# Seven slots of stationary weights and seven low-part slots, moved within 256 bytes of SBUF

## The chip, the cores and the metric

The kernel runs on one NeuronCore of one Trainium2 chip; the other cores are idle. The metric is the device time of one execution in microseconds, as the median of repeated runs. All inputs and outputs are float32 in device memory.

## The reference: what is computed

One hybrid decoder layer for a sequence of 1024 tokens and a model width of 1024:

```
h = x + W_out( concat[ sliding-window attention heads with sinks | forgetting-attention heads ] )
        both head groups read RMSNorm(x) through one combined input projection
y = h + W_down( relu( W_up RMSNorm(h) )^2 )        W_up: 1024 x 4096, W_down: 4096 x 1024
```

## The kernel before

**Numbers in two parts.** TensorE multiplies in a reduced form of float32 (`float32r`). To keep float32 accuracy every operand is split into a high part (a rounded copy) and a low part (the rest), by `split` (lines 75 to 80): one engine makes the copy, another one the difference. A product of two operands is then three matmuls into one PSUM bank: high x high, high x low and low x high. A matmul instruction has a *stationary* operand (128 columns, brought in by its own weight load, LDWEIGHTS) and a *moving* operand (up to 512 columns). Every matmul of the profile has its own weight load, also where two in a row use the same weights.

**The stages.** First the input projection for part of the heads (tile `qps`, moving 384 columns), then the attention with the remaining projections threaded in between (tiles `ps`, moving 384 or 392 columns), then the output projection (`po`, moving 512), then the up projection (`pu`, moving 512) and the down projection (`pd`, moving 512). Up and down are done by Strassen-Winograd's scheme: seven products of half-size blocks instead of eight.

**The up stage** (`up`, line 1060, called for j = 0 to 15 from line 1298). For each j it takes sums and differences of four blocks of raw weights (`wur`, `wus`) on VectorE, and then, for the seven products in the order `UP = (1, 2, 3, 6, 7, 5, 4)`, it splits that product's weights into a slot `wu` and multiplies:

```
w = w_slot("wu", [2, 4, P], F32R)
split(w[:, 0], w[:, 1], src[n], nc.scalar, nc.vector if n in (2, 6, 5) else nc.gpsimd)
for k in range(4):
    mm(m[n], w[:, 0, k], bh[n][:, k], k == 0, False)
    mm(m[n], w[:, 0, k], bl[n][:, k], False, False)
    mm(m[n], w[:, 1, k], bh[n][:, k], False, k == 3)
```

So a product is 12 matmuls: four triples, each of high weights x high part, high weights x low part, low weights x high part. Seven products by 16 steps by 12 make 1344 matmuls. The moving operands `bh[n]` and `bl[n]` are made once in the output stage and stay. The weights go through seven slots `w0` to `w6` in turn (`w_slot`, line 1054, with `nw` starting at 4). Because there are seven products and seven slots, each product meets the same slot in every step: product 1 uses w5, 2 uses w6, 3 uses w0, 6 uses w1, 7 uses w2, 5 uses w3 and 4 uses w4.

**The slots.** All of these buffers come from `slot` (line 146): a named place in a pool that is given out again and again. Pool `zw` (tags w0 to w6, 4096 bytes per partition each, and two buffers `wor` of 2048 bytes) lies above pool `zl` (tags m0 to m5, r0, r1, 8192 bytes each); pool `zr` (tags c0 to c13, 8192 bytes each, then `rr` and `tmp`) lies at the other end of SBUF. Inside a pool the places follow each other in the order in which the tags are first asked for; for `zw` this is w2, w4, w3, wor twice, w0, w1, w5, w6. Tags c0, c2, ... c12 hold the high parts `bh[n]`, and c1, c3, ... c13 the low parts `bl[n]`. All these sizes are whole multiples of 256 bytes, so before the change every one of these slots starts at the same place modulo 256 bytes (224), and so do the inner pieces of a slot that matmuls read, which lie multiples of 512 bytes apart.

The slots have other users too. In the output stage w0 and w1 hold the split output weights `wos` (`out_weights`, line 870), w2 and w3 the tiles `xt` and `h`, w4 the tiles `pc` and `b12`. In the down stage w0 to w6 receive the raw hidden rows `hr` by DMA (line 1200), c0 to c9 the raw weights `wda`, c10 to c13 two of the first four pairs `hx`, `wx` of split operands (`FIRST`, line 1149: `hx` in c10 and c12, `wx` in c11 and c13), and later the sums of the results.

**One stage whose low part lies elsewhere.** In `w_tiles` (line 178) the projection weights, which are the moving operand there, have their low part 384 x 4 = 1536 bytes after the high part where 384 columns are loaded, a multiple of 256; where 392 columns are loaded it lies 400 x 4 = 1600 bytes after it, 64 bytes off a multiple of 256:

```
lo = 384 if n == 384 else 400
return wr, w[:, :n], w[:, lo : lo + n]
```

The order of the instructions on each engine is chosen when the program is built, by a planner with a cost model; waits between engines follow from which tiles are read and written. Pools are opened with `reuse_waits="tile"`: a tile that takes over bytes of an earlier tile waits for that tile's last users.

Of the kernel before, what the change touches and what calls it, by code (L numbers as in the profile page):

```python
# [16 lines left out]
P = 128  # L17
# [38 lines left out]
def hybrid_layer(  # L56
# [86 lines left out]
        tc.tile_pool(name="zl", bufs=1, side="left", reuse_waits="tile")  # L143
    )}

    def slot(tag, name, shape, dt=F32, pool=None):
        pool = o[pool or ("zw" if tag[0] == "w" else "zl")]
        return pool.tile([P] + shape, dt, tag=tag, name=name, bufs=1)


    X = [
        [slot(tag, "x", [2, 2, 512], F32R) for tag in tags]
        for tags in (("m1", "m2", "m3", "m4"), ("m0", "r0", "r1", "m5"))
    ]
# [705 lines left out]
    def mix_tiles(e):  # L860
        m = mixt[e] = slot(MIX[e], f"mix{e}", [2, S], F32R)
        mh[e], ml[e] = m[:, 0, :], m[:, 1, :]
# [7 lines left out]
    def out_weights(dt, e0):  # L870
        i = nout[0] = nout[0] + 1
        wr = o["zw"].tile([P, 4, P], F32, tag="wor", name="wor", bufs=2)
        nc.sync.dma_start(wr, w_o[dt][:, e0 : e0 + 4, :])
        w = slot(f"w{i % 2}", "wos", [2, 4, P], F32R)
        split(w[:, 0], w[:, 1], wr, nc.scalar, nc.gpsimd)
        return w[:, 0], w[:, 1]
# [154 lines left out]
    for dt in (1, 5, 2, 6, 3, 7):  # L1031
        w = out_weights(dt, 4)
# [273 lines left out]
    for i in range(len(STEPS)):  # L1306
        down(i)
        if STEPS[i][0] == len(PHASES) - 1 and late:
            name, dt, cs = late.pop(0)
# [65 lines left out]
```

## Time and profile before

| what | before |
|---|---|
| median of three runs | 1091.47 us (1091.2 to 1092.87) |
| span of the profiled execution, first to last instruction | 1090.4 us |
| what lies around the span, taken as median less span | 1.1 us |
| TensorE matmul busy | 1080.1 us, 99% of the span |
| weight loads busy (beside the matmuls) | 933.8 us, 86% |
| VectorE / ScalarE / GpSimd busy | 782.7 / 571.4 / 362.4 us |
| up stage, first to last start of a matmul | 473.7 to 780.8 us |
| granted TensorE clock | 0.999 |

The profiled execution's own device time is not listed apart from its span. Matmuls are pipelined: a row's duration of one matmul (some 390 ns) is longer than the distance from its start to the next one's start, and it is this distance that adds up to the time. It is read by dividing a stretch by the number of weight loads or matmuls that start in it.

### The profile page before, as it was taken

How to read it: one execution, taken by the hardware profiler on the slowest of the kernel's cores; microseconds unless marked ns; L12 is line 12 of the kernel's file. 1: busy time of each engine (PE TensorE's matmuls, PEld its weight loads, DVE VectorE, ACT ScalarE, POOL GpSimd, SP SyncE). 2: the span in 40 equal slices, each digit the busy share in tenths (PEclk: the TensorE clock that was granted, in tenths of full speed). 3: DMA queues.
4: the chain of work that ended last, by engine and by line, in shares of the span. 5: the costliest groups of instructions: out<-in, count | busy, mean ns of one | idle time of the engine just before them, and what ended most of it. 6: DMA issues, size and time to landing. Idle time of an engine off the chain costs nothing.

```text
span 1090.4 us, 15675 instructions
## 1 busy us (share of the span) xinstructions
PE 1080.1 (99%) x5556; PEld 933.8 (86%) x5556; DVE 782.7 (72%) x1321; ACT 571.4 (52%) x1022; POOL 362.4 (33%) x352
## 2 busy tenths in 40 slices
PE   9999999999999999999999999999999999999998
PEld 8999999999898888778888888888888888888886
DVE  8377677765776786898686869867665876674395
ACT  5558588776667766554545444353633433333331
POOL 4572523434445543333222232322212222231100
PEclk9999999999999999999999999999999999999999
DMA  9401212324657564663554543443998876665523
GB/s 292 156 22 53 69 36 65 113 70 150 230 164 252 182 209 173 212 231 126 193 184 174 188 160 135 149 170 145 335 390 308 305 288 224 237 231 177 176 87 116
DMA packets 96223, 195.69 MB, mean 179 GB/s; under 512 B 7392, under 2 KB 19856, under 8 KB 96144
## 3 DMA queue, kind: packets, MB, share of 16 engines
q1 hardware_dynamic: 95856, 194.54, 51.0%
q8 instruction: 44, 0.72, 0.3%
q14 instruction: 35, 0.29, 0.1%
q10 hardware_dynamic: 288, 0.15, 0.0%
HBM read 141.61 MB, written 53.04 MB: 179 GB/s over the span
## 4 chain that ended last, share of the span: by engine, by line
PE 86%; DMA 5%; DVE 4%; ACT 1%; issue 1%; POOL 1%; SPq 0%; DVEq 0%; ACTq 0%; POOLq 0%
PE pd L73 28%; PE pu L73 27%; PE ps L73 13%; PE po L73 4%; PE spb L73 3%; PE pvb L73 3%; PE tpb L739 3%; PE sp L73 1%; PE pv L73 1%; PE tpa L568 1%; DMA h_d<-h 1%; DMA xq<-in_x_dram 1%; DMA wr<-in_w_a_dram 1%; DMA rd_d<-rd 1%; PE ptk L334 1%
## 5 line engine op out<-in xcount | busy, mean ns | idle before, releaser
L73 PE MATMUL pd<-hx,wx 128*128 128x512 f32 (+1 forms) x1350 | 304.9, 388 | 0.0
L73 PEld LDWEIGHTS pd<-hx,wx 128*128 128x128 f32 x1350 | 252.7, 188 | 52.2
L73 PE MATMUL pu<-bh,wu 128*128 128x512 f32 x896 | 276.6, 390 | 0.3 <-POOL wu L80 0.2
L73 PEld LDWEIGHTS pu<-bh,wu 128*128 128x128 f32 x896 | 168.0, 188 | 36.1 <-POOL wu L80 0.6
L73 PE MATMUL ps<-w,x 128*128 128x384 f32 (+1 forms) x960 | 198.3, 344 | 0.5 <-ACT z L463 0.3
L73 PE MATMUL pu<-bl,wu 128*128 128x512 f32 x448 | 174.0, 389 | 0.0
L73 PEld LDWEIGHTS ps<-w,x 128*128 128x128 f32 x960 | 164.8, 189 | 3.8 <-ACT z L463 0.7
L77 ACT CAST hx<-hr 128x1024 fp32r<-128x1024 f32 x56 | 59.1, 1055 | 176.1 <-PE pd L73 170.9
L80 POOL TENSOR_TENSOR wx<-wda,wx 128x1024 fp32r<-128x1024 f32 x24 | 64.3, 2678 | 196.6 <-ACT wx L77 188.6
L80 DVE TENSOR_TENSOR hx<-hr,hx 128x1024 fp32r<-128x1024 f32 x56 | 72.5, 1302 | 72.5 <-ACT hx L77 72.5
L73 PEld LDWEIGHTS pu<-bl,wu 128*128 128x128 f32 x448 | 84.1, 188 | 17.7 <-issue 0.2
L73 PE MATMUL po<-mix,wos 128*128 128x512 f32 x384 | 94.2, 395 | 0.6 <-ACT pc L914 0.3
L73 PEld LDWEIGHTS po<-mix,wos 128*128 128x128 f32 x384 | 70.6, 188 | 15.7 <-ACT wos L77 1.1
L80 POOL TENSOR_TENSOR wu<-wus,wu 128x512 fp32r<-128x512 f32 x32 | 46.6, 1459 | 111.8 <-ACT wu L77 99.5
L80 POOL TENSOR_TENSOR wu<-wur,wu 128x512 fp32r<-128x512 f32 x32 | 44.1, 1378 | 102.7 <-ACT wu L77 100.1
L1047 DVE TENSOR_TENSOR ht<-hb 128x512 f32<-128x512 f32 x32 | 22.9, 757 | 62.8 <-ACT hb L1102 62.8
L80 POOL TENSOR_TENSOR w<-wr,w 128x384 fp32r<-128x384 f32 (+1 forms) x47 | 50.1, 1074 | 40.1 <-ACT w L77 28.6
L77 ACT CAST wu<-wus 128x512 fp32r<-128x512 f32 x64 | 37.9, 618 | 46.5 <-PE pu L73 39.2
L77 ACT CAST wx<-wda 128x1024 fp32r<-128x1024 f32 x56 | 58.5, 1049 | 6.8 <-DMA wda<-in_w_d_dram 6.5
L703 ACT ACTIVATE sb<-sb,nmb 128x128 f32<-128x128 f32 (+3 forms) x64 | 49.7, 778 | 22.1 <-DVE nmb L697 21.6
L406 DVE TENSOR_TENSOR ptl<-tpb,pth 128x512 fp32r<-128x512 f32 (+1 forms) x80 | 49.6, 631 | 15.1 <-ACT pth L405 14.3
L1101 ACT ACTIVATE hb<-hb 128x2048 f32<-128x2048 f32 x16 | 30.7, 1917 | 48.5 <-DVE hb L1050 48.4
(211 smaller groups left out, 1844.5 us busy)
## 6 DMA issues: line engine op xcount, KB each, us to landing
wda<-in_w_d_dram SPq DMA_DIRECT2D x34, 1024.0 KB, 8.7
hr<-hid_d SPq DMA_DIRECT2D x56, 512.0 KB, 5.7
wur<-in_w_u_dram SPq DMA_DIRECT2D x32, 512.0 KB, 4.4
hid_d<-ht SPq DMA_DIRECT2D x16, 1024.0 KB, 4.5
hid_d<-hb SPq DMA_DIRECT2D x16, 768.0 KB, 3.6
mix<-mixs_d SPq DMA_DIRECT2D x7, 1024.0 KB, 5.4
wr<-in_w_b_dram SPq DMA_DIRECT2D x32, 192.0 KB, 2.5
xq<-in_x_dram SPq DMA_DIRECT2D x8, 512.0 KB, 5.9
```

What stands on the lines that cost most here:

```text
L73: return nc.tensor.matmul(out, lhsT, rhs, start=start, stop=stop)
L77: hi_eng.copy(hi, src)
L80: lo_eng.tensor_tensor(out=lo, in0=src, in1=hi.bitcast(F32), op=ALU.subtract)
L334: nc.tensor.transpose(pt[:w, j * P : (j + 1) * P], x[:, 4 * c + j, col : col + w], ident)
L406: nc.vector.tensor_tensor(out=lo[:, cols], in0=pt[:, cols], in1=hi[:, cols].bitcast(F32), op=ALU.subtract)
L568: nc.tensor.transpose(tp[:, hh * P : (hh + 1) * P], pts[hh // 2][:, hh % 2, c0 : c0 + P], ident)
L703: nc.scalar.activation(pr[:, :nk], pr[:, :nk], AF.Exp, scale=-1.0, bias=nm[:, c : c + 1], accum_out=dn_b[p % 2][:, h, i : i + 1] if p < 3 ...
L739: nc.tensor.transpose(tp[:, c0 : c0 + P], probs[qi][:, kb * P : (kb + 1) * P], ident)
L1047: eng.tensor_tensor(out=out, in0=a, in1=b, op=ALU.subtract)
L1101: nc.scalar.activation(b, b, AF.Relu)
```

## The change

Four of the seven weight slots and all seven low-part slots become a little larger than what is put into them, and the contents start a little behind the slot's start:

```
+    SHIFT = {
+        "w4": 2, "w3": 4, "w1": 4, "w5": 4,
+        "c1": 16, "c3": 16, "c5": 16, "c7": 16, "c9": 16, "c11": 16, "c13": 16,
+    }
+
     def slot(tag, name, shape, dt=F32, pool=None):
         pool = o[pool or ("zw" if tag[0] == "w" else "zl")]
-        return pool.tile([P] + shape, dt, tag=tag, name=name, bufs=1)
+        if tag not in SHIFT:
+            return pool.tile([P] + shape, dt, tag=tag, name=name, bufs=1)
+        n, by = math.prod(shape), SHIFT[tag]
+        full = 1024 + 8 if tag[0] == "w" else 2048 + 64
+        t = pool.tile([P, full], dt, tag=tag, name=name, bufs=1)[:, by : by + n]
+        if len(shape) == 1:
+            return t
+        if len(shape) == 2:
+            return t.rearrange("p (a b) -> p a b", b=shape[1])
+        return t.rearrange("p (a b c) -> p a b c", b=shape[1], c=shape[2])
```

A shifted w slot is 32 bytes larger, so what follows it in the pool moves by 32 bytes. Modulo 256 bytes the slots then start, in their order in the pool, at: w2 224, w4 232 (8 bytes in), w3 16, w0 32, w1 48, w5 80, w6 96. A shifted c slot is 256 bytes larger and its contents start 64 bytes in: the low parts lie at 32 modulo 256, the high parts stay at 224. No instruction is added or taken away, none changes its shape, and each slot keeps its name, its number of buffers and its users.

## The prediction

> **What bounds the kernel now.** I read the page's header, the granted clock and the busy shares first, then the waits of TensorE.
>
> ```profile
> span 1090.4 us, 15675 instructions
> PE 1080.1 (99%) x5556; PEld 933.8 (86%) x5556; DVE 782.7 (72%) x1321; ACT 571.4 (52%) x1022; POOL 362.4 (33%) x352
> ...
> core 0: 1090.4 us, clock 0.999
> ...
> engine line waited for: us in total, times, longest us
> PE qps L73 <- DVE warm L191: 1.3, 1, 1.3
> ...
> PE pu L73 <- POOL wu L80: 0.2, 1, 0.2
> ```
>
> TensorE is busy for 99% of the span at a full clock. Its longest wait for another engine is 1.3 us, and in the up stage it waits 0.2 us in all for a split weight. So the time is the number of matmuls times the distance between two starts, and a change of places counts only by what it does to that distance. The next view is the instructions that touch the tile `wu`, then the weight loads in order of time, merged, for three stretches without a break: `qps` with 384 columns, `pd` with 512, and `ps` with 392. The last row is the up stage by windows.
>
> ```profile
> engine op xcount: duration ns min/median/max, first and last start us, forms
> L73 PEld LDWEIGHTS pu<-bh,wu x896: 186/188/190, 473.5 to 780.5; 128*128 128x128 f32 x180
> L73 PE MATMUL pu<-bh,wu x896: 388/389/793, 473.7 to 780.8; 128*128 128x512 f32 x180
> ...
> L73 PE MATMUL pu<-bl,wu x448: 387/389/396, 473.9 to 780.5; 128*128 128x512 f32 x150
> ```
>
> ```profile
> 10.91 27.75 PEld L73 LDWEIGHTS qps<-w,x 128*128 128x128 f32 x160
> ...
> 800.03 135.96 PEld L73 LDWEIGHTS pd<-hx,wx 128*128 128x128 f32 x600
> ...
> 43.35 6.95 PEld L73 LDWEIGHTS ps<-w,x 128*128 128x128 f32 x39
> ...
> 490.00:626.00 136.00, 136.00 (x602) 112.65 (x600) 103.58 (x149) 63.55 (x86) 39.76 (x29) 1.00 0.46 171
> ```
>
> A row of n weight loads lasts n - 1 distances and one load of 188 ns. For 384 columns that is (27.75 - 0.19) / 159 = 173.3 ns; for 512 in the down stage (135.96 - 0.19) / 599 = 226.7 ns; in the up stage 136.00 / 600 = 226.7 ns. The two sizes give a slope of 53.3 ns / 128 = 0.417 ns per column and a fixed part of 13.3 ns per matmul. By that rule 392 columns take 163.3 + 13.3 = 176.7 ns; measured is (6.95 - 0.19) / 38 = 177.9 ns, with some 0.3 ns of uncertainty since the row gives hundredths of a microsecond. This is the one stretch in which the low part lies 64 bytes off the high part modulo 256, by `lo = 400` in line 183. In the two others stationary and moving operands all lie at one place modulo 256.
>
> The up stage is then 1344 x 226.7 = 304.6 us of the 307.3 us from the first matmul at 473.7 to the one behind the last (780.8 + 0.2); 2.7 us are breaks at its start and in its middle. After a break the distance isn't at once 226.7 ns. The matmuls behind the one in step 10, in order of time:
>
> ```profile
> 666.30 0.79 PE L73 MATMUL pu<-bh,wu 128*128 128x512 f32 x1
> 666.93 0.40 PE L73 MATMUL pu<-bl,wu 128*128 128x512 f32 x1
> 667.17 0.63 PE L73 MATMUL pu<-bh,wu 128*128 128x512 f32 x2
> 667.63 0.39 PE L73 MATMUL pu<-bl,wu 128*128 128x512 f32 x1
> ...
> 669.02 0.39 PE L73 MATMUL pu<-bl,wu 128*128 128x512 f32 x1
> ```
>
> From 666.93 to 669.02 there are nine distances, 2.09 us, so 232 ns each: 5.5 ns more than in the settled stream, 50 ns until it has settled. The same operands at the same places thus cost 5.5 ns more when the stream isn't in step. I read the fixed 13.3 ns as partly a matter of how the reads of moving and stationary operand fall against each other, and that is what the change shifts.
>
> **The change part by part.** *Instructions.* None is added, removed or moved; the pools grow by 4 x 32 and 7 x 256 bytes per partition. Cost 0 by itself.
>
> *The low parts' shift.* 448 of the 1344 matmuls stream a low part that now lies 64 bytes off, just as in the 392-column stretch, with a triple in the same order: high, low, high. That stretch pays 177.9 - 176.7 = 1.2 ns per matmul on the average of its triple. For 1344 matmuls this is 1.6 us, if the excess comes from the 64 bytes. It may also come from the 392 columns themselves, which no other stretch has; then it is 0. The trace can't tell these apart. I take the half, **0.8 us**.
>
> *The seven stationary places.* Only product 7 (slot w2, at 224) keeps its place. For the six others no row shows a stationary operand elsewhere than at 224 beside a float32 moving operand of 512. Below, the whole fixed part could go: 13.3 ns for 6/7 of 1344 = 1152 matmuls, 15.4 us less. Above, the stream could stay out of step all the time: 5.5 ns x 1152 = 6.3 us more. The nearest row is the 392-column one, where operands do lie at two places, and its distance differs by about 1 ns from the rule. So I take 0 for them beside the 0.8 us above, and keep both ends.
>
> *The switches.* Every 12 matmuls the stationary operand goes to another place, 16 x 7 = 112 times. If the stream falls out of step each time and settles in nine matmuls, this is 112 x 50 ns = 5.6 us; if it slides over, 0. In the 392-column stretch the moving place alternates two times in three matmuls for at most 3.7 ns per triple, so a switch costs some 2 ns there: 112 x 2 ns = **0.2 us**.
>
> *Output and down stage.* Their slots move too: `wos` now lies at 32 and 48, and two `wx` at 32.
>
> ```profile
> L73 PE MATMUL po<-mix,wos 128*128 128x512 f32 x384 | 94.2, 395 | 0.6 <-ACT pc L914 0.3 <-ACT wos L77 0.3
> L73 PE MATMUL pd<-hx,wx 128*128 128x512 f32 x1338 | 303.4, 389 | 0.0
> ```
>
> That is at most 384 + 48 matmuls, against 1152; they are taken at 0 like those, with ends by their share of 432 / 1152: -5.8 to +2.4 us.
>
> *VectorE, ScalarE, GpSimd, DMA.* Splits write to the moved slots, and `hr` is loaded into them by DMA.
>
> ```profile
> L77 ACT CAST wu<-wus x64: 601/620/629, 472.2 to 759.4; 128x512 fp32r<-128x512 f32 x64
> L80 POOL TENSOR_TENSOR wu<-wus,wu x32: 1291/1426/1911, 477.8 to 757.5; 128x512 fp32r<-128x512 f32 x32
> ...
>   PE pu L73: 54.2, 29
> ...
> hr<-hid_d SPq DMA_DIRECT2D x56, 512.0 KB, 5.7
> ...
>   PE pd L73: 170.9, 49
> ```
>
> Seven slots give a split a lead of several products of 12 x 226.7 = 2.7 us; ScalarE in its turn sits idle 54.2 us until TensorE frees a slot of `wu` and 170.9 us in the down stage. A split of 0.62 + 1.43 us would have to become several times longer before TensorE waited: 0. A load of 5.7 us is issued as soon as its slot is free, so a few per cent more there cost 0 as well. If this cover were gone, each microsecond of delay per product would cost 112 us, but nothing here is near that.
>
> **Sum.** 0.8 + 0.2 + 0 = 1.0 us more than the profiled span of 1090.4, so 1091.4 us; with the 1.1 us that lie between span and median the time is 1091.47 + 1.0 = **1092.4 us**.
>
> **A rule of the skill against the trace.** The Trainium skill, page "TensorE: Matmul & The Clock Gate", section "Step-by-step: what each phase is for", says that TensorE has two independent read ports, so loading the next weights takes nothing from the running matmul's reads. By it no place could matter and the sum would be 0: 1091.5 us, the first rival below. The 232 ns of the unsettled stream and the 177.9 ns of the 392 columns speak against a strict reading of it, though neither proves that it is the place.
>
> The same page, section "Wait — 56ns, not 53.3ns?", measures 215.7 ns for 512 columns back to back, with no fresh weights. By that the most that places could win in the up stage is an estimated 1344 x 11 ns = 14.8 us, 1076.7 us.
>
> **The rivals.**
>
> *R1, places do nothing.* The distance stays 226.7 ns for every product: 1091.5 us. For it: the same 226.7 ns stands in the up and the down stage though the tiles lie many kilobytes apart. Against it: the 392-column row. It is the same verdict as my forecast.
>
> *R2, the stream falls out of step (slower).* The place is TensorE's reads in the up stage; seven stationary places against two moving ones leave no common rhythm, and the distance goes from 226.7 ns towards the 232 ns that follow a break. At 2 ns per matmul and above it decides the verdict; with half of the 5.5 ns it is 1344 x 2.75 = 3.7 us, 1095.2 us, with all of it 7.4 us, 1098.9 us. For it: the settled rhythm stands only where all places are alike, and 392 columns are above the rule. Against it: 392 columns, with two places, are nearer to settled than to unsettled.
>
> *R3, unlike places collide less (faster).* If the 13.3 ns come largely from both reads starting at the same place modulo 256, moving six of seven products apart takes a part away: a quarter of it, 3.3 ns x 1344 = 4.5 us, gives 1087.0 us; half, 6.7 ns, 9.0 us, gives 1082.5 us. For it: the fixed part is there in every stretch in which all places are alike. Against it: nothing in the trace shows a distance of settled 512-column matmuls below 226.7, and the one mixed stretch lies above.
>
> *R4, the change misses its place*: the planner orders instructions otherwise, or a slot that now overlaps another old tile waits for it. 32 bytes to 1.8 KB of shift reach at most one neighbouring tile, whose users are the finished attention; a stop there costs one product of 2.7 us plus 50 ns of settling, so 1094.2 us.
>
> **How the numbers follow.** What a measurement of this kernel can tell from no change is about 0.2%, 2.2 us, or 1.6 ns for each of 1344 matmuls. My forecast and R1 together, within that: 0.43. R2: 0.25 and R4 0.04, both slower, with 0.02 for the slower edge of the forecast: 0.31. R3: 0.26. The time is that of the forecast, 1092.4 us. Its own range is 1090.0 to 1094.0. The whole range goes down to a quarter of the fixed part (1087.0) and up to half-way between R2's two prices, 1344 x 4.1 ns = 5.5 us, 1097.0; outside lie the deep end of R3 with 0.12 and the high end of R2 with 0.07.
>
> **What would show it.** In the profile after: 600 loads of the down stage should still last 136.0 us. In the up stage the distance should be read product by product, since each has its slot: product 7 (224) shows the low parts' shift alone, products 3, 1 and 2 those of 32, 80 and 96, product 6 48, product 5 16, product 4 232. Right would be 226 to 229 ns in each, low passes not all equal to high ones, and an up stage of 307 to 310 us. R2 would show 229 to 232 ns in most products; R3 223 or less in those away from 224, with product 7 unchanged. A stage of up that begins later than 473.7 us would be R4, or the output stage's moved `wos`. My reading as a whole is wrong if products differ by more than 5 ns from each other, for then it is the place itself and not the rhythm that sets the price.

## The result and the profile after

The changed kernel takes 1100.49 us in the median (1098.99 to 1100.92, 3 runs) against 1091.47 us: a ratio of 1.0079 with a 95% interval from 1.0059 to 1.0098, 9.0 us more. The span of its profiled execution is 1098.8 us against 1090.4.

Every engine runs the same instructions in the same order in both programs, so all of it is in how long they take. This is all that TensorE waits for in the changed kernel's up stage:

```profile
PE pu L73 <- ACT bh L990: 0.3, 1, 0.3
```

The changed kernel's rows of the tiles `po`, `pu` and `pd` (shortest, median and longest duration in ns, then first and last start in us):

```profile
L73 PE MATMUL po<-mix,wos x384: 387/394/507, 332.0 to 474.3; 128*128 128x512 f32 x192
L73 PE MATMUL pu<-bh,wu x896: 387/394/800, 474.5 to 788.7; 128*128 128x512 f32 x180
L73 PE MATMUL pu<-bl,wu x448: 387/394/401, 474.8 to 788.5; 128*128 128x512 f32 x150
L73 PE MATMUL pd<-hx,wx x1350: 278/389/398, 788.9 to 1093.9; 128*128 128x512 f32 x192, 128*128 128x256 f32 x1
```

And its windows in the up and the down stage (length, then busy time and instructions of TensorE's matmuls, its weight loads, VectorE, ScalarE and GpSimd, then the granted clock, the busy share of the DMA engines and their GB/s):

```profile
500.00:620.00 120.00, 120.00 (x518) 97.09 (x517) 85.33 (x127) 61.62 (x78) 33.68 (x26) 1.00 0.52 187
820.00:940.00 120.00, 120.00 (x531) 99.41 (x530) 83.56 (x67) 46.20 (x48) 31.17 (x11) 1.00 0.79 285
```

The same tile rows of the kernel before (`pu` stands in the prediction), and its windows:

```profile
L73 PE MATMUL po<-mix,wos x384: 387/389/499, 332.4 to 473.5; 128*128 128x512 f32 x192
L73 PE MATMUL pd<-hx,wx x1350: 278/389/389, 781.0 to 1085.6; 128*128 128x512 f32 x192, 128*128 128x256 f32 x1
```

```profile
500.00:620.00 120.00, 120.00 (x531) 99.41 (x530) 87.58 (x127) 60.64 (x80) 35.08 (x27) 1.00 0.51 187
820.00:940.00 120.00, 120.00 (x531) 99.38 (x530) 80.55 (x63) 46.58 (x50) 32.30 (x12) 1.00 0.75 275
```

In 120 us of the up stage TensorE starts 517 weight loads in place of 530: 232.1 ns from start to start in place of 226.4, with the clock at 1.00 and no wait for another engine of more than 0.3 us. In the down stage it is 530 both times. From first to last start the up stage takes 314.2 us (474.5 to 788.7) against 307.1, the output stage 142.3 against 141.1, the down stage 305.0 against 304.6. That is 7.1 + 1.2 + 0.4 us more, and 0.4 us less ahead of the output stage: 8.3 of the 8.4 us between the spans. The single parts below tell which slots did it beside the up stage: with the low parts alone the output stage is 141.0 and the down stage 305.0 us, with the stationary places alone they are 142.6 and 304.6 us.

By product, each distance counted to the product of the matmul that it starts with, and without the few distances over 300 ns in which the stream breaks, the starts in the trace give:

| product | slot at, after | ns per matmul, before | after |
|---|---|---|---|
| 7 | 224 | 226.8 | 232.1 |
| 4 | 232 | 226.7 | 235.2 |
| 5 | 16 | 226.7 | 231.0 |
| 3 | 32 | 226.7 | 234.3 |
| 6 | 48 | 226.7 | 231.3 |
| 1 | 80 | 226.9 | 231.0 |
| 2 | 96 | 227.0 | 230.8 |
| mean of all | | 226.8 | 232.2 |

All seven are dearer, also product 7, whose slot did not move; its low part did.

### The profile page after: what moved, and what is told of

It is laid out like the page before. It is cut to its first block, busy times and chain, and to the rows that moved or that the text cites. A ratio compares the mean times of both kernels' runs of the same rounds, so it can differ in the third digit from the quotient of the medians.

```text
span 1098.8 us, 15675 instructions
## 1 busy us (share of the span) xinstructions
PE 1088.7 (99%) x5556; PEld 934.7 (85%) x5556; DVE 769.8 (70%) x1321; ACT 575.6 (52%) x1022; POOL 360.6 (33%) x352
## 4 chain that ended last, share of the span: by engine, by line
PE 87%; DVE 5%; DMA 4%; ACT 2%; issue 1%; POOL 1%; SPq 0%; ACTq 0%; DVEq 0%; POOLq 0%
PE pu L73 28%; PE pd L73 27%; PE ps L73 11%; PE po L73 5%; PE spb L73 4%; PE pvb L73 3%; PE tpb L753 3%; PE pv L73 1%; PE tpa L582 1%; PE sp L73 1%; DMA xq<-in_x_dram 1%; DMA xr<-in_xT_dram 1%; PE ptk L348 1%; DMA h_d<-h 1%; POOL sq L298 0%
## 5 line engine op out<-in xcount | busy, mean ns | idle before, releaser
L73 PE MATMUL pu<-bh,wu 128*128 128x512 f32 x896 | 281.7, 395 | 0.3 <-ACT bh L990 0.3
L80 POOL TENSOR_TENSOR wu<-wus,wu 128x512 fp32r<-128x512 f32 x32 | 49.4, 1547 | 129.1 <-ACT wu L77 129.1
L80 POOL TENSOR_TENSOR wu<-wur,wu 128x512 fp32r<-128x512 f32 x32 | 41.7, 1302 | 91.3 <-ACT wu L77 91.3
L419 ACT CAST pth<-tpb 128x512 fp32r<-128x512 f32 (+1 forms) x80 | 42.0, 543 | 24.1 <-PE tpb L753 18.7
```

Of the source, the lines that this page charges most:

```text
L73: return nc.tensor.matmul(out, lhsT, rhs, start=start, stop=stop)
L80: lo_eng.tensor_tensor(out=lo, in0=src, in1=hi.bitcast(F32), op=ALU.subtract)
L419: nc.scalar.copy(hi[:, cols], pt[:, cols])
```

## The experiments

Five theories were open. **A**: any unlikeness of places takes the stream out of its rhythm. **B** and **C**: the stationary places alone, or the low parts alone, do it. **D**: a constant relation settles, only changes cost. **E**: each place of the stationary operand relative to the moving one has a settled price of its own.

### The low parts alone

The changed kernel with the entries of the weight slots left out of `SHIFT`:

```
+    SHIFT = {"c1": 16, "c3": 16, "c5": 16, "c7": 16, "c9": 16, "c11": 16, "c13": 16}
```

> Only the seven low-part slots are moved (to 32 modulo 256 bytes); all seven stationary slots stay at 224. The changed kernel's up stage has 232.2 ns from matmul start to matmul start where the kernel before has 226.8. Theory A (any unlikeness of places, moving or stationary, takes the stream out of its rhythm): still 230 to 233 ns in the up stage, 1096 to 1100 us. Rival B (the seven unlike stationary places and the switches between them do it): back to 227 ns, 1091 to 1093 us. Rival C (the low parts alone do it): 231 to 233 ns, 1097 to 1100 us; A and C are told apart by the next run.

Measured: 1097.81 us against 1090.87 us of the kernel before on the same chip, ratio 1.0064 (1.0049 to 1.0079). The windows of the weight loads alone (length, busy time and count, then clock, DMA share and GB/s), first the up, then the down stage:

```profile
500.00:620.00 120.00, 97.09 (x518) 1.00 0.52 189
820.00:940.00 120.00, 99.38 (x530) 1.00 0.78 286
```

518 loads in 120 us are 231.7 ns; over the whole stage the mean is 232.0 ns. The low parts alone are enough, and all three passes of a triple are dearer (233, 232 and 231 ns in the median), not the low one only. B alone falls.

### The stationary places alone

The changed kernel with the entries of the low-part slots left out:

```
+    SHIFT = {"w4": 2, "w3": 4, "w1": 4, "w5": 4}
```

> Only the seven stationary slots are moved (16, 32, 48, 80, 96, 224, 232); high and low moving parts all stay at 224. Theory A (any unlikeness): 230 to 233 ns in the up stage, 1096 to 1100 us, with product 7 (slot at 224, like its moving parts) the best. Rival B (the stationary places): the same 232 ns, but here all of the loss. Rival C (the low parts alone): 227 ns, 1091 to 1093 us.

Measured: 1098.18 us against the same 1090.87 us, ratio 1.0066 (1.0051 to 1.0081). The up stage's window:

```profile
500.00:620.00 120.00, 97.33 (x519) 1.00 0.50 186
```

231.2 ns: this half is enough too, so C alone falls as well. The halves don't add: 5.2 ns for the one, 5.1 ns for the other, 5.5 ns for both. Product 7, alike again, is back at 227.8 ns, with 231 and 232 ns (medians) in the first and the last of its twelve matmuls and 227 between; the six others lie at 231.3 to 233.5 ns.

### All stationary slots together, 64 bytes ahead, then 64 bytes behind

```
-        return pool.tile([P] + shape, dt, tag=tag, name=name, bufs=1)
+        if tag != "w2":
+            return pool.tile([P] + shape, dt, tag=tag, name=name, bufs=1)
+        t = pool.tile([P, 1024 + 16], dt, tag=tag, name=name, bufs=1)[:, 16 : 16 + math.prod(shape)]
...
```

w2 is the first slot of its pool, so the others move with it (in the second kernel by 48 elements, 192 bytes, in place of 16). The edit is made to the kernel before, and nothing changes from product to product here.

> All seven stationary slots are moved together by 64 bytes (to 32), all moving parts stay at 224, so stationary and moving place are unlike but nothing changes from product to product. Theory A (unlikeness breaks the rhythm): 230 to 233 ns, 1096 to 1100 us. Rival D (a stream settles at any constant relation; only changes from matmul to matmul or product to product cost): 227 ns after some ten matmuls, 1091 to 1093 us. Rival E (each relation of stationary to moving place has a settled price of its own): a steady number other than 226.7, either way; then some relation may be better than before.

Measured: 1101.0 us against 1090.87 us, ratio 1.0093 (1.0076 to 1.0109), dearer than the change itself. The up stage's window:

```profile
500.00:620.00 120.00, 96.70 (x515) 1.00 0.51 188
```

233.0 ns in the window, 233.3 ns in every product, and settled: after the first few, the distances go 231, 235, 231, 236, 231, 235 without end. D falls: a constant relation does settle, but at another price. A is missed by little here, 0.3 ns and 1 us above its ranges. The second kernel was run after the streams below, with its price read off them:

> All seven stationary slots are moved together by 192 bytes (to 160), the moving parts stay at 224: the stationary operand lies 64 bytes behind the moving one modulo 256, not 64 ahead as in the run that moved it by 64. The streams alone measured 228.9 ns for this relation against 233.3 ns for the other and 226.7 ns for alike places. Theory E (each relation has its settled price, read off the streams): 228.9 ns in every product of the up stage, 1344 x 2.2 = 3.0 us more than before there, and 360 x 2.2 = 0.8 us more in the output stage; 1094 to 1096 us. Theory A (any unlikeness costs about the same 5 ns): 231 to 234 ns, 1098 to 1101 us.

Measured: 1096.13 us against 1091.01 us, ratio 1.0043 (1.0029 to 1.0057).

```profile
500.00:620.00 120.00, 98.47 (x525) 1.00 0.52 188
```

120 / 525 is 228.6 ns, and the mean over the stage 228.9 ns, in every product between 228.8 and 229.0. That is E's number to 0.1 ns, and outside of A's. The time in all came out 0.1 us above E's 1094 to 1096 us.

### The streams alone

> Nothing of the layer is computed: streams of 36 to 168 matmuls with their own weight loads, one after the other, no other engine at work, one stream for each relation of places. Streams a: the stationary place moved against both moving parts; b: all at one place; c: the low moving part alone moved; d: both moving parts moved; e and f: other column counts, with all alike (e) and the low part 64 bytes off (f); g: places switched every twelve matmuls. Theory A: 226.7 ns in every b and in a at 0, 230 to 233 ns in the other a, in c and d and in both seven-place streams. Rival D: 226.7 ns in all of a, b and d, more in c and in the seven-place streams. Rival E: different steady numbers in a, from under 220 to over 235 ns. If the 392 columns' 1.2 ns come from the 64 bytes, stream e with 392 columns has 176.7 ns and f 177.9; if they come from the columns, both have 177.9.

The core of this kernel is one call per matmul, with `w` and `m` the places under test in bytes, `k` a multiple of 512 bytes, and `st` and `mv` buffers that lie multiples of 4096 bytes apart:

```
nc.tensor.matmul(
    b[:, :cols], st[:, w // 4 + k : w // 4 + k + 128], mv[:, m // 4 : m // 4 + cols],
    start=i % 12 == 0, stop=i % 12 == 11 or i == count - 1,
)
```

It took 546.6 us. While the streams run no other engine works: this is the window of the trace that holds nearly all of them, in the columns of the first windows above.

```profile
18.00:531.00 513.00, 513.00 (x2317) 427.72 (x2316) 0.00 (x0) 0.00 (x0) 0.00 (x0) 1.00 0.00 1
```

Its weight loads in order of time, merged by stream (start and length in us, then the count). The number in a name is the distance in bytes, or the count of columns for e and f: a is the stationary operand moved, b all at one place, c the low moving part moved, d both moving parts moved, e all alike and f the low moving part moved by 64 at another count of columns. The streams g change the stationary place every twelve matmuls: gsevenl goes through the seven places with the low part moved, gtwo goes to and fro between alike and 64 bytes ahead.

```profile
18.78 7.44 PEld L102 LDWEIGHTS a0w<-zone,zone 128*128 128x128 f32 x33
26.26 7.89 PEld L102 LDWEIGHTS a16w<-zone,zone 128*128 128x128 f32 x35
...
50.99 8.35 PEld L102 LDWEIGHTS a64w<-zone,zone 128*128 128x128 f32 x36
...
118.03 8.20 PEld L102 LDWEIGHTS a192w<-zone,zone 128*128 128x128 f32 x36
...
201.17 8.23 PEld L102 LDWEIGHTS b16s<-zone,zone 128*128 128x128 f32 x36
...
217.66 8.15 PEld L102 LDWEIGHTS b64s<-zone,zone 128*128 128x128 f32 x36
...
275.31 8.29 PEld L102 LDWEIGHTS c64l<-zone,zone 128*128 128x128 f32 x36
...
333.58 8.30 PEld L102 LDWEIGHTS d128m<-zone,zone 128*128 128x128 f32 x36
...
362.89 6.40 PEld L102 LDWEIGHTS e392n<-zone,zone 128*128 128x128 f32 x36
369.27 6.41 PEld L102 LDWEIGHTS f392l<-zone,zone 128*128 128x128 f32 x36
...
450.81 38.98 PEld L102 LDWEIGHTS gsevenl<-zone,zone 128*128 128x128 f32 x168
...
508.90 22.11 PEld L102 LDWEIGHTS gtwo<-zone,zone 128*128 128x128 f32 x96
```

As in the prediction, a row of n loads lasts n - 1 distances and 0.19 us. Alike is (7.44 - 0.19) / 32 = 226.6 ns; 64 bytes ahead is (8.35 - 0.19) / 35 = 233.1 ns, 64 bytes behind (192 ahead) 228.9 ns. These rows contain the few matmuls that a stream needs to settle; the settled numbers, from the last fifteen starts of each stream or a whole number of repeats, are:

| stationary ahead of both moving parts, bytes | settled ns at 512 columns |
|---|---|
| 0, 16, 240 | 226.7 |
| 192 | 228.9 |
| 176 | 230.0 |
| 24 / 8 / 4 | 230.0 / 230.6 / 232.5 |
| 80 | 232.0 |
| 32, 40, 48, 64, 72, 112, 128, 144, 160, 208, 224 | 233.3 |
| 96 | 234.4 |

No other engine works in this kernel while the streams run, and the clock is 1.00, so this is TensorE's own affair. A falls: 16 bytes to either side cost nothing, though the places are unlike. E stands, with a smaller spread than it was given: the settled prices in the table reach only from 226.7 to 234.4 ns. The place as such matters little: all alike at any tried multiple of 32 bytes settles at 226.7 ns, while 16 bytes off a multiple of 32 it is 230.0. What counts is mainly the relation, and none tried here is cheaper than alike. Moving both moving parts ahead by 64 or 192 gives 228.9 and 233.3 ns, as the same relation modulo 256 does with the stationary operand moved (192 and 64). One pair does not agree: d128m settles at some 232 ns, while the stationary operand moved by 128 gives 233.3. So the relation modulo 256 isn't quite the whole account.

The table explains the kernel with moved places product by product. Slots 16, 32, 48, 80, 96, 224 and 232 lie 48, 64, 80, 112, 128, 0 and 8 bytes ahead of 224. The table has 233.3, 233.3, 232.0, 233.3, 233.3, 226.7 and 230.6 for them, 231.8 in the mean; that kernel's products measured 232.8, 233.3, 231.5, 232.6, 233.5, 227.8 and 231.3, 231.8 in the mean. So in this order switching every twelve matmuls costs next to nothing. It isn't free everywhere: gtwo takes (22.11 - 0.19) / 95 = 230.7 ns, where the mean of its two prices is 230.0. The stream that goes through the seven places with the low part moved, as the changed kernel does, has (38.98 - 0.19) / 167 = 232.3 ns, the kernel 232.2.

At 392 columns alike places take (6.40 - 0.19) / 35 = 177.4 ns, and with the low part 64 bytes off 177.7.

### Everything alike at another place

The 64-byte shift of the stationary slots as above, and `rr` made larger by 48 elements. Its pool `zr` lies at the right end of SBUF, so the slots ahead of `rr` go down by 192 bytes, and all moving slots of the up stage come to the same place, 224 - 192 = 32:

```
-    rr = o["zr"].tile([P, S], F32, name="rr")
+    rr = o["zr"].tile([P, S + 48], F32, name="rr")[:, :S]
```

> All seven stationary slots and all fourteen moving slots lie at 32 modulo 256 bytes: another place than before, but the same one for both operands of the up stage. Theory E (the price hangs on the place of the stationary operand relative to the moving one; alike costs 226.7 ns at 512 columns): an up stage of 306 us with 226.7 ns, as before. Rival (the place 32 as such is dear): 231 to 233 ns and an up stage of 313 us. The output stage keeps its stationary weights at 32 against moving operands at 224, for which theory E asks 233.3 ns in place of 226.7 in 360 matmuls, up to 2.4 us more; so 1091 to 1094 us in all by theory E, 1100 us by the rival.

Measured: 1092.23 us against 1091.36, ratio 1.0008 (0.9999 to 1.0018).

```profile
500.00:620.00 120.00, 99.38 (x530) 1.00 0.52 188
```

530 loads in 120 us again, as before the change. The same stationary slots at 32 that cost 8.0 us in the up stage beside moving parts at 224 cost nothing beside moving parts at 32. So in the whole kernel, too, it is the relation and not the place 32 as such. The output stage, whose weights lie at 32 beside moving parts that did not go with them, is 142.7 us against 141.1 before, as in the kernel with the 64-byte shift alone (142.5).

### Looking for a relation that is better than alike

> Nothing of the layer is computed: streams of 24 matmuls as in the first set of streams, now also with the low stationary part at a place of its own (p..a, p..b, p..c), with stationary and low moving part both moved (p..d, p..e), and the same relations at 256 (m) and 384 columns (k). If alike places are the cheapest relation at 512 columns, no stream goes under 226.7 ns there; if some combination avoids more of the meetings, it goes to 220 ns or less and a kernel built on it is worth a run. At 256 columns a low part 64 bytes off took 117.8 ns against 120.0 for alike places, so there a cheaper relation than alike is expected, at 384 columns none under 173 ns.

It took 499.43 us. The same view of two of its streams: p240a has only the low stationary part moved, by 240 bytes at 512 columns; m64f has the stationary operand 64 ahead at 256 columns.

```profile
68.74 5.41 PEld L142 LDWEIGHTS p240a<-zone,zone 128*128 128x128 f32 x24
...
383.01 2.79 PEld L142 LDWEIGHTS m64f<-zone,zone 128*128 128x128 f32 x24
```

None of the 65 combinations at 512 columns settles under 226.7 ns, and four come down to it: the low stationary part alone moved by 16 or 240 bytes, or by 16 or 48 with the low moving part as far the other way. At 384 columns none is under 173.3. At 256 columns it is otherwise: most of the fourteen settle below the 120.0 ns of alike places, at 117 to 119 ns, and m64f is the lowest with (2.79 - 0.19) / 23 = 113.0 ns, settled 113.3. The kernel before has its 512-column streams of the output, up and down stage in the cheapest relation that was found (226.7 ns), so no faster version came out of this for them. Its matmuls of 256 columns stand in the attention between others; moving their operands was not tried.

## Why the prediction was wrong, point by point

**What bounds the kernel** held: the time went with the distance between starts, and with nothing else. No wait came up and the order of instructions stayed, so R4 did not happen; the up stage begins 0.8 us later because the output stage ahead of it got longer.

**The low parts' shift, 0.8 us.** This step failed, in its row. It priced 448 moved matmuls by the 392-column stretch, as the half of an excess of 1.2 ns. The streams show that there the excess comes mostly from the columns, alike or not (177.4 against 177.7 ns), and that a shift of 64 bytes that costs 0.3 ns at 392 columns costs 5.3 ns at 512 (232.0 settled). The nearest row by place was not near by shape. Alone, this part makes the stage 232.0 - 226.8 = 5.2 ns dearer per matmul, 7.0 us for 1344, against 0.8.

**The seven places, taken at 0.** This step failed the same way: it followed from "operands do lie at two places, and its distance differs by about 1 ns". Measured alone it is 5.1 ns per matmul, 6.8 us. The upper end, 5.5 ns for each of the six moved products, was passed as well: with the places alone they take 232.5 ns in the mean, 5.7 more than 226.8. A stream 64 ahead pays 6.7 ns, product 4 in the changed kernel 8.5. The two parts were also treated as a sum, and they are not.

**The switches, 0.2 us,** were right to be small: in the kernel with moved places the mean with switches equals the mean of the settled prices.

**Output and down stage, taken at 0,** were low: 1.2 and 0.4 us, inside the ends of -5.8 to +2.4. The output weights now lie at 32 and 48. Late in that stage, over sixty distances without a break, the mean goes from 226.7 to 232.4 ns; over the whole stage, whose stream breaks in 47 places in both kernels, it goes only from 228.6 to 232.2, because the stream before is often unsettled there.

**VectorE, ScalarE, GpSimd and DMA at 0** was right: the largest wait of the up stage is 0.3 us.

**The rivals.** R2 named the place, the sign and, at its full price of 7.4 us in the up stage, nearly the size (7.1 us; the time is 1.6 us past its 1098.9, and the other stages grew by as much); it got 0.25, and its high end was left out of the range, which ended at 1097.0. Its mechanism was wrong in one point: nothing falls out of step. The streams settle, at dearer distances. That these lie near the 232 ns behind a break is a likeness of numbers that no run explains, so that R2 met the size may be luck. R3 had the sign backwards: both operands at the same place is among the cheapest relations at 512 columns, not one that leaves something to win. The sign that was to upset its reading, products more than 5 ns apart, was just missed in the changed kernel, where they differ by up to 4.4 ns, and came in the kernel with moved places, with 5.7 (227.8 to 233.5). The streams then showed what it stood for: the place sets the price, not a lost rhythm.

The page "TensorE: Matmul & The Clock Gate" of the Trainium skill, section "Step-by-step: what each phase is for", says that loading the next weights takes nothing from the running matmul's reads. The streams disagree if that is read as "places don't matter": with TensorE alone at work the distance goes from 226.7 to over 233 ns with the relation of the two places. What in the memory or in TensorE makes it so, no run here shows.

## What to carry to other kernels

Keep the stationary and the moving operand of a long float32 matmul stream of 512 columns at the same place modulo 256 bytes, by slot sizes that are multiples of 256 bytes, and look at this again when a pool gets an odd-sized tile: here 2 to 3% of each 512-column matmul hung on it. When one row of a trace is to price something that no other row shows, ask first whether it has the same shape; the shift that cost 0.3 ns at 392 columns cost 5.3 ns at 512, and one run of streams alone measured both. Two shifts that each cost 5 ns can cost 5.5 ns together, so halves of such a change aren't added.

## What the runs showed of the hardware

Many settled distances are whole multiples of 6.67 ns: 113.3, 120.0, 173.3, 180.0 (400 columns), 226.7 and 233.3 ns are 17, 18, 26, 27, 34 and 35 of them, and where the distances alternate in threes, as in 228.9 (230, 231, 226), the three together are 103 times 6.67 ns. At 400 columns alike places settle on such a multiple; 392 took 177.4 ns alike, where the straight line through 384 and 512 gives 176.7. Why this is so, no run shows.

The best relation hangs on the column count: 64 bytes ahead costs 6.7 ns more than alike at 512 columns, 1.5 ns more at 384 (174.8 against 173.3) and 6.7 ns less at 256. A stationary operand 16 bytes to either side of the moving one costs nothing at 512 columns, 8 bytes ahead cost 3.9 ns.
